# Gate and up products of a chunk as one block product, with a seven-product scheme in two of eight pairs of k tiles

## The chip, the cores and the metric

The kernel runs on one core of one Trainium2 chip. The metric is device microseconds (us) of one execution, lower is better. The engines named below are PE (matrix products; PEld is its weight load), DVE (vector), ACT (scalar), POOL and SP, whose queue here issues nearly all DMAs.

## The reference, cut to what matters

One decoder layer for 256 positions and 2048 channels: a gated feed-forward block (FFN), a mixer of two attention branches, and a second FFN. The change touches only the two FFNs, of which each computes

```python
def swiglu(h, w_gate, w_up, w_down):
    return (jax.nn.silu(h @ w_gate) * (h @ w_up)) @ w_down

x = x + 0.5 * swiglu(rms_norm(x, ffn1_norm), ffn1_w_gate, ffn1_w_up, ffn1_w_down)
```

with h of 256 x 2048, w_gate and w_up of 2048 x 5632, w_down of 5632 x 2048, all in float32.

## The kernel before

**Number format.** A product of float32 matrices is made of three PE products. Each operand is split in two parts of the type float32r: hi is the value copied to that type (ACT, line 98 for weights), lo is the value less hi (DVE, line 99). The product is then hi\*hi + hi\*lo + lo\*hi, three matmuls into the same PSUM tile (lines 114, 115 and 116). The x operand is split once per FFN (xh, xl, held with k along the partitions), the weights are split as they arrive.

**Tiles.** A k tile is 128 rows of a weight. A weight load (line 96, on SP's queue) brings two k tiles of 512 columns into one `raw` tile of 512 KB; four `raw` buffers exist (RAW_BUFS). A split pair (`w_hi`, `w_lo`) covers one `raw` tile; five such pairs exist (SPL_BUFS). One group is one such pair: two k tiles times two blocks of 128 positions (t = 0, 1) times three matmuls, so 12 matmuls of 128 x 128 weights (a block of x is the stationary operand) by 512 moving columns.

**An FFN.** `ffn` walks over 11 chunks of 512 columns of the gate and up weights in two halves (6 and 5 chunks). For each chunk, `linear` runs over the 8 groups of the gate weight into two PSUM tiles `mm` (one for each t), ACT applies Silu to them (line 254), `linear` runs over the 8 groups of the up weight into two more, and DVE multiplies both (line 258). `turn_blocks` then brings the result into k-major form: two DVE transposes (line 158), a DMA to DRAM (`blocks`, line 160) and one back (`moved`, line 163). Eight groups later (`defer(BLOCK_WAIT, ...)`) `split_blocks` splits it into `ah` and `al` (ACT line 131, DVE line 132). After a half's chunks, four `linear` calls with the down weight use `ah` and `al`.

**Order.** Each engine runs its own queue in the order that the framework fixed when the kernel was built; the framework also adds all waits between engines. A tile's buffer is reused once its last reader has finished. PSUM has eight banks: `ps_mm` four, `ps_tr` two, `ps_s` two.

Of the kernel before, what the change touches and what calls it, by code (L numbers as in the profile page):

```python
# [11 lines left out]
F32 = mybir.dt.float32  # L12
# [17 lines left out]
GRP = 2  # L30
RAW_BUFS = 4
SPL_BUFS = 5
HALVES = (6, 5)
DIL_G, DIL_H = 3, 4
DIFF_H = 4
# [16 lines left out]
def hybrid_layer_kernel(ctx: ExitStack, tc: tile.TileContext, a: dict, out: bass.AP):  # L52
# [23 lines left out]
    def tick():  # L76
        nonlocal groups
        groups += 1
        while later and later[0][0] <= groups:
            heapq.heappop(later)[2]()  # L80

    def flush():
        while later:
            heapq.heappop(later)[2]()

    def weight_groups(w, n0, nk):

        nonlocal last_hi, last_lo
        for k0 in range(0, nk, GRP):
            raw = wraw.tile([P, GRP, CH], F32, name="raw")  # L90
            hi = wspl.tile([P, GRP, CH], F32R, name="w_hi")
            lo = wspl.tile([P, GRP, CH], F32R, name="w_lo")
            step = 1 if groups == 0 else GRP
            for g in range(0, GRP, step):
                ks = slice(g, g + step)
                nc.sync.dma_start(raw[:, ks], w[(k0 + g) * P:(k0 + g + step) * P, n0:n0 + CH]  # L96
                                  .rearrange("(k p) n -> p k n", p=P))
                last_hi = nc.scalar.activation(hi[:, ks], raw[:, ks], AF.Copy)  # L98
                last_lo = nc.vector.tensor_tensor(lo[:, ks], raw[:, ks], hi[:, ks].bitcast(F32), op=ALU.subtract)  # L99
            yield k0, hi, lo  # L100

    def linear(w, n0, xh, xl, nk, ahead=None):

        ps = [ps_mm.tile([P, CH], F32, name="mm") for _ in range(NT)]
        for k0, hi, lo in weight_groups(w, n0, nk):
# [10 lines left out]
                    nc.tensor.matmul(ps[t], xl[:, k, sl], hi[:, kk], start=False, stop=k == nk - 1)  # L116
            tick()
        return ps

    def rsqrt_mean(ss, n, cols):  # L120

# [114 lines left out]
        return [rsqrt_mean(total(ss[t]), D, 1) for t in range(NT)]  # L236

    def ffn(wg, wu, wd, norm, done, ahead=None):
        with tc.tile_pool(name="act", bufs=1) as apool, tc.tile_pool(name="actw", bufs=2) as aw, \
                tc.tile_pool(name="actb", bufs=1) as bp:  # L240
            ah = apool.tile([P, 4 * HALVES[0], S], F32R, name="ah")
            al = apool.tile([P, 4 * HALVES[0], S], F32R, name="al")
            rs = None
            j = 0
            for half, count in enumerate(HALVES):
                down = wd[j * CH:(j + count) * CH]
                for i in range(count):
                    ps = linear(wg, j * CH, xh, xl, KD, ahead if j == 0 else None)
                    if rs is None:
                        rs = norm()  # L250
                    sg = []
                    for t in range(NT):
                        s = aw.tile([P, CH], F32, name="sg")
                        nc.scalar.activation(s, ps[t], AF.Silu, scale=rs[t])  # L254
                        sg.append(s)
                    ps = linear(wu, j * CH, xh, xl, KD)
                    for t in range(NT):
                        nc.vector.scalar_tensor_tensor(sg[t], ps[t], rs[t], sg[t], op0=ALU.mult, op1=ALU.mult)
                    x = turn_blocks(sg, bp)
                    defer(BLOCK_WAIT, lambda x=x, i=i: split_blocks(x, ah, al, 4 * i))  # L260
                    j += 1
                for n in range(D // CH):
                    ps = linear(down, n * CH, ah, al, 4 * count)
                    (done if half else part)(n, ps, bp)

    def part(n, ps, _):
# [461 lines left out]
```

## Time and profile before

| | us |
|---|---|
| median of 3 runs | 2147.96 (2147.25 to 2148.06) |
| the profiled execution | 2147.71 |
| its span in the profile | 2145.9 |
| PE busy in the span | 2133.2 |
| DVE busy | 1226.7 |
| ACT busy | 993.5 |

The span is what the profile covers; the profiled execution took 1.8 us more than its span. Busy times are sums over an engine's instructions. The granted clock of PE is full (1.00) in every stretch of this run. Matmul records overlap in time, because matmuls are pipelined, so the pace of matmuls is read from the distance between their starts and not from the length of one record.

### The profile page before, as it was taken

How to read it: one execution, taken by the hardware profiler on the slowest of the kernel's cores; microseconds unless marked ns; L12 is line 12 of the kernel's file. 1: busy time of each engine (PE TensorE's matmuls, PEld its weight loads, DVE VectorE, ACT ScalarE, POOL GpSimd, SP SyncE). 2: the span in 40 equal slices, each digit the busy share in tenths (PEclk: the TensorE clock that was granted, in tenths of full speed). 3: DMA queues.
4: the chain of work that ended last, by engine and by line, in shares of the span. 5: the costliest groups of instructions: out<-in, count | busy, mean ns of one | idle time of the engine just before them, and what ended most of it. 6: DMA issues, size and time to landing. Idle time of an engine off the chain costs nothing.

```text
span 2145.9 us, 25034 instructions
## 1 busy us (share of the span) xinstructions
PE 2133.2 (99%) x9490; PEld 1766.7 (82%) x9490; DVE 1226.7 (57%) x1456; ACT 993.5 (46%) x1193; POOL 47.7 (2%) x50
## 2 busy tenths in 40 slices
PE   8999999999999999999999999999999999999999
PEld 6888888888888888888888888888888888888887
DVE  5655554455556666767755566665555544555553
ACT  6445443444445545555556444454444433444442
POOL 0000000000000011010100000000000000000000
PEclk9999999999999999999999999999999999999999
DMA  7676665666667767666654567666666655676663
GB/s 251 215 230 216 215 214 191 193 216 212 219 216 245 246 196 234 227 215 213 205 181 157 196 222 244 220 226 215 210 223 215 223 192 193 198 229 212 213 230 134
DMA packets 241662, 456.25 MB, mean 213 GB/s; under 512 B 14162, under 2 KB 37252, under 8 KB 241284
## 3 DMA queue, kind: packets, MB, share of 16 engines
q1 hardware_dynamic: 241152, 454.09, 64.3%
q0 software_dynamic: 288, 0.53, 0.2%
q8 instruction: 74, 1.21, 0.2%
q14 instruction: 48, 0.39, 0.1%
q10 hardware_dynamic: 100, 0.03, 0.0%
HBM read 428.89 MB, written 25.69 MB: 212 GB/s over the span
## 4 chain that ended last, share of the span: by engine, by line
PE 99%; DMA 0%; DVE 0%; SPq 0%; issue 0%
PE mm L114 33%; PE mm L115 32%; PE mm L116 32%; PE s L581 0%; DMA xs<-in_x_dram 0%; PE tr L144 0%; PE s L500 0%; PE tr L610 0%; PE s L534 0%; PE tr L599 0%; PE tr L611 0%; PE tr L547 0%; DVE xs L695 0%; PE tr L522 0%; SPq L96 0%; SPq L225 0%
## 5 line engine op out<-in xcount | busy, mean ns | idle before, releaser
L99 DVE TENSOR_TENSOR w_lo<-raw,w_hi 128x1024 fp32r<-128x1024 f32 (+1 forms) x769 | 932.6, 1220 | 761.3 <-ACT w_hi L98 759.7
L98 ACT ACTIVATE w_hi<-raw 128x1024 fp32r<-128x1024 f32 (+1 forms) x769 | 807.8, 1057 | 910.1 <-PE mm L116 854.5
L114 PE MATMUL mm<-w_hi,xh 128*128 128x512 f32 x2144 | 837.0, 391 | 0.0
L115 PE MATMUL mm<-w_lo,xh 128*128 128x512 f32 x2144 | 836.4, 390 | 0.0
L116 PE MATMUL mm<-w_hi,xl 128*128 128x512 f32 x2144 | 833.9, 390 | 0.0
L116 PEld LDWEIGHTS mm<-w_hi,xl 128*128 128x128 f32 x2144 | 402.8, 188 | 83.5
L115 PEld LDWEIGHTS mm<-w_lo,xh 128*128 128x128 f32 x2144 | 402.8, 188 | 83.1
L114 PEld LDWEIGHTS mm<-w_hi,xh 128*128 128x128 f32 x2144 | 402.6, 188 | 83.1
L114 PE MATMUL mm<-w_hi,ah 128*128 128x512 f32 x704 | 273.9, 389 | 0.0
L115 PE MATMUL mm<-w_lo,ah 128*128 128x512 f32 x704 | 273.9, 389 | 0.0
L116 PE MATMUL mm<-w_hi,al 128*128 128x512 f32 x704 | 273.9, 389 | 0.0
L115 PEld LDWEIGHTS mm<-w_lo,ah 128*128 128x128 f32 x704 | 132.1, 188 | 27.5
L114 PEld LDWEIGHTS mm<-w_hi,ah 128*128 128x128 f32 x704 | 132.1, 188 | 27.5
L116 PEld LDWEIGHTS mm<-w_hi,al 128*128 128x128 f32 x704 | 132.1, 188 | 27.4
L132 DVE TENSOR_TENSOR al<-moved,ah 128x512 fp32r<-128x512 f32 x44 | 28.6, 688 | 75.2 <-ACT ah L131 75.2
L125 POOL TENSOR_TENSOR rr<-rv,mhalf 128x4 f32<-128x4 f32 (+1 forms) x34 | 41.6, 1226 | 1302.0 <-DVE rv L123 1302.0
L131 ACT ACTIVATE ah<-moved 128x512 fp32r<-128x512 f32 x44 | 25.4, 624 | 89.3 <-DMA moved<-blocks 89.3
L114 PE MATMUL mm<-w_hi,yh 128*128 128x512 f32 x128 | 49.9, 390 | 0.0
L116 PE MATMUL mm<-w_hi,yl 128*128 128x512 f32 x128 | 49.8, 389 | 0.0
L115 PE MATMUL mm<-w_lo,yh 128*128 128x512 f32 x128 | 49.8, 389 | 0.0
L158 DVE STREAM_TRANSPOSE turned<-sg 128x512 f32<-128x512 f32 x44 | 48.3, 1097 | 0.0
L254 ACT ACTIVATE sg<-mm,rr 128x512 f32<-128x512 f32 x44 | 29.8, 689 | 19.9 <-PE mm L116 19.9
(150 smaller groups left out, 750.6 us busy)
## 6 DMA issues: line engine op xcount, KB each, us to landing
raw<-in_w_in_dram SPq DMA_DIRECT2D x184, 512.0 KB, 3.6
raw<-in_ffn_w_up_dram SPq DMA_DIRECT2D x176, 512.0 KB, 4.6
raw<-in_ffn_w_down_dram SPq DMA_DIRECT2D x176, 512.0 KB, 4.5
raw<-in_ffn_w_gate_dram SPq DMA_DIRECT2D x175, 512.0 KB, 3.8
blocks<-turned SPq DMA_DIRECT2D x41, 512.0 KB, 4.4
raw<-in_w_out_dram SPq DMA_DIRECT2D x32, 512.0 KB, 5.2
moved<-blocks SPq DMA_DIRECT2D x31, 512.0 KB, 5.1
raw<-in_w_diff_branch_dram SPq DMA_DIRECT2D x16, 512.0 KB, 4.7
```

The source lines that it names most:

```text
L98: last_hi = nc.scalar.activation(hi[:, ks], raw[:, ks], AF.Copy)
L99: last_lo = nc.vector.tensor_tensor(lo[:, ks], raw[:, ks], hi[:, ks].bitcast(F32), op=ALU.subtract)
L114: nc.tensor.matmul(ps[t], xh[:, k, sl], hi[:, kk], start=k == 0, stop=False)
L115: nc.tensor.matmul(ps[t], xh[:, k, sl], lo[:, kk], start=False, stop=False)
L116: nc.tensor.matmul(ps[t], xl[:, k, sl], hi[:, kk], start=False, stop=k == nk - 1)
L125: nc.gpsimd.tensor_tensor(r, v, mhalf[:, :cols], op=ALU.pow)
L131: nc.scalar.activation(hi, src, AF.Copy)
L132: nc.vector.tensor_tensor(lo, src, hi.bitcast(F32), op=ALU.subtract)
L158: nc.vector.transpose(r[:, :, t], srcs[t].rearrange("p (kt i q) -> p q kt i", i=32, q=4))
L254: nc.scalar.activation(s, ps[t], AF.Silu, scale=rs[t])
```

## The change

Chunks 1 to 10 of each FFN no longer run gate and up one after the other: `two_chunks` takes the pair of gate and up columns (index i), the two blocks of positions (t) and the two k tiles of a pair (k) as a product of 2 x 2 by 2 x 2 blocks. There are eight pairs u = 0 to 7 of k tiles in a chunk. In six of them the eight block products are made as before, into four PSUM accumulators c00, c01, c10, c11 (first index t, second i), with three matmuls for each block product (`three`). In the pairs WINO = (3, 5) seven block products are made instead (p1, p5, p6, p7 go to four accumulators of their own, the others to c00, c01, c10), of sums and differences of blocks. The sums of x blocks are made once per FFN (`sums_of_x`), the sums of weight blocks (`t_a`, `t_b`) in each such pair, by DVE from `raw`, before they are split by `parts` like any weight. After pair 5, p1, p5, p6 and p7 are combined into e, u2, x, y, and at the end of the chunk the four c are added to these. All eight PSUM banks are in use; which four hold the c alternates from chunk to chunk. Silu now comes after the chunk's end, for both t. Chunk 0 runs as before. In the FFNs a sixth split pair exists (FFN_SPL).

```diff
+FFN_SPL = 1
+WINO = (3, 5)
...
+    def parts(src, n=GRP):
+        nonlocal last_hi, last_lo
+        hi, lo = split_tiles()
+        last_hi = nc.scalar.activation(hi[:, :n], src, AF.Copy)
+        last_lo = nc.vector.tensor_tensor(lo[:, :n], src, hi[:, :n].bitcast(F32), op=ALU.subtract)
+        return hi, lo
...
+    def three(ps, xs, ws, start, stop):
+        (h, l), (wh, wl) = xs, ws
+        nc.tensor.matmul(ps, h, wh, start=start, stop=False)
+        nc.tensor.matmul(ps, h, wl, start=False, stop=False)
+        nc.tensor.matmul(ps, l, wh, start=False, stop=stop)
...
+    def two_chunks(j, cols, xh, xl, nk, sx, tmp):
+        four = [ps_mm.tile([P, CH], F32, name="mm") for _ in range(4)]
+        def other():
+            tr = [ps_tr.tile([P, 2, S], F32, name="tr").rearrange("p a b -> p (a b)") for _ in range(2)]
+            sc = ps_s.tile([P, 2, CH], F32, name="s")
+            return [*tr, sc[:, 0], sc[:, 1]]
+        (c00, c01, c10, c11), (p1, p5, p6, p7) = (four, other()) if j % 2 else (other(), four)
...
+            if u not in sx:
+                for i in range(2):
+                    hi, lo = parts(raw[i])
+                    for k in range(2):
+                        for t in range(NT):
+                            three(c[t][i], op(k, t), (hi[:, k], lo[:, k]), u == 0 and k == 0, u == nu - 1 and k == 1)
+                    tick()
+                continue
...
+            b = parts(raw[0])
+            ta, tb = wtmp.tile([P, GRP, CH], F32, name="t_a"), wtmp.tile([P, GRP, CH], F32, name="t_b")
+            nc.vector.tensor_tensor(ta[:, 0], raw[1][:, 0], raw[0][:, 0], op=ALU.subtract)
+            nc.vector.tensor_tensor(ta[:, 1], raw[1][:, 0], raw[1][:, 1], op=ALU.subtract)
+            three(p1, op(0, 0), part(b, 0), st, sp)
+            three(c00, op(1, 0), part(b, 1), False, False)
+            b = parts(raw[1][:, 1:], 1)
+            three(c01, sm(3), part(b, 0), False, False)
+            nc.vector.tensor_tensor(tb[:, 0], raw[1][:, 1], ta[:, 0], op=ALU.subtract)
+            nc.vector.tensor_tensor(tb[:, 1], raw[0][:, 1], tb[:, 0], op=ALU.subtract)
+            tick()
+            b = parts(ta)
+            three(p5, sm(0), part(b, 0), st, sp)
+            three(p7, sm(2), part(b, 1), st, sp)
+            b = parts(tb)
+            three(p6, sm(1), part(b, 0), st, sp)
+            three(c10, op(1, 1), part(b, 1), False, False)
+            tick()
+            if sp:
+                nc.scalar.activation(e, p1, AF.Copy)
+                nc.vector.tensor_tensor(u2, p6, e, op=ALU.add)
+                nc.vector.tensor_tensor(x, p5, u2, op=ALU.add)
+                nc.vector.tensor_tensor(u2, p7, u2, op=ALU.add)
+                nc.vector.tensor_tensor(y, p7, x, op=ALU.add)
+        for acc, p in ((e, c00), (u2, c10), (x, c01), (y, c11)):
+            nc.vector.tensor_tensor(acc, p, acc, op=ALU.add)
+        return (e, x), (u2, y)
...
+                    if j == 0:
+                        ps = linear(wg, 0, xh, xl, KD, ahead)
+                        rs = norm()
...
+                        up = linear(wu, 0, xh, xl, KD)
+                        sx = sums_of_x(sxp, WINO)
+                    else:
+                        out = two_chunks(j, ((wg, j * CH), (wu, j * CH)), xh, xl, KD, sx, aw)
+                        sg, up = [o[0] for o in out], [o[1] for o in out]
+                        for t in range(NT):
+                            nc.scalar.activation(sg[t], sg[t], AF.Silu, scale=rs[t])
```

## Rows read from the trace of the kernel before

**Rows 1.** The page: span, busy time of engines, and the chain's shares by engine

```profile
span 2145.9 us, 25034 instructions
PE 2133.2 (99%) x9490; PEld 1766.7 (82%) x9490; DVE 1226.7 (57%) x1456; ACT 993.5 (46%) x1193; POOL 47.7 (2%) x50
PE 99%; DMA 0%; DVE 0%; SPq 0%; issue 0%
```

**Rows 2.** Waits of PE, whole span (us in total, times, longest)

```profile
PE tr L144 <- DMA xs<-in_x_dram: 4.5, 2, 4.3
PE tr L210 <- DMA g_raw<-in_ffn_norm_dram: 3.9, 1, 3.9
```

**Rows 3.** PE timeline in an FFN chunk: start us, length us

```profile
99.78 0.39 PE L114 MATMUL mm<-w_hi,xh 128*128 128x512 f32 x1
...
101.82 0.39 PE L114 MATMUL mm<-w_hi,xh 128*128 128x512 f32 x1
...
102.50 0.39 PE L114 MATMUL mm<-w_hi,xh 128*128 128x512 f32 x1
```

**Rows 4.** DVE groups by line and form: count, busy us, mean ns, idle before

```profile
L99 DVE TENSOR_TENSOR w_lo<-raw,w_hi 128x1024 fp32r<-128x1024 f32 x767 | 931.2, 1221 | 758.7 <-ACT w_hi L98 757.2
L158 DVE STREAM_TRANSPOSE turned<-sg 128x512 f32<-128x512 f32 x44 | 48.3, 1097 | 0.0
L258 DVE SCALAR_TENSOR_TENSOR sg<-mm,rr,sg 128x512 f32<-128x512 f32 x44 | 30.9, 742 | 0.0
L132 DVE TENSOR_TENSOR al<-moved,ah 128x512 fp32r<-128x512 f32 x44 | 28.6, 688 | 75.2 <-ACT ah L131 75.2
L446 DVE TENSOR_TENSOR q<-ra,rb 128x128 f32<-128x128 f32 x20 | 5.6, 280 | 0.0
L656 DVE TENSOR_TENSOR y<-mm,sig 128x512 f32<-128x512 f32 x8 | 5.1, 681 | 0.0
```

**Rows 5.** ACT groups by line and form, same columns

```profile
L98 ACT ACTIVATE w_hi<-raw 128x1024 fp32r<-128x1024 f32 x767 | 806.6, 1059 | 906.6 <-PE mm L116 854.5 <-DMA raw<-in_w_in_dram 25.7 <-DMA raw<-in_ffn_w_down_dram 6.6
L254 ACT ACTIVATE sg<-mm,rr 128x512 f32<-128x512 f32 x44 | 29.8, 689 | 19.9 <-PE mm L116 19.9
L131 ACT ACTIVATE ah<-moved 128x512 fp32r<-128x512 f32 x44 | 25.4, 624 | 89.3 <-DMA moved<-blocks 89.3
```

**Rows 6.** Timeline of DVE after a chunk: start us, length us, count, idle before

```profile
145.10 1.40 DVE L258 SCALAR_TENSOR_TENSOR sg<-mm,rr,sg 128x512 f32<-128x512 f32 x2
146.42 1.08 DVE L158 STREAM_TRANSPOSE turned<-sg 128x512 f32<-128x512 f32 x1
147.43 1.18 DVE L99 TENSOR_TENSOR w_lo<-raw,w_hi 128x1024 fp32r<-128x1024 f32 x1
148.53 1.10 DVE L158 STREAM_TRANSPOSE turned<-sg 128x512 f32<-128x512 f32 x1
...
161.70 3.50 DVE L99 TENSOR_TENSOR w_lo<-raw,w_hi 128x1024 fp32r<-128x1024 f32 x3 [0.18 <-ACT w_hi L98]
```

**Rows 7.** Timeline of ACT in the same stretch

```profile
153.69 1.06 ACT L98 ACTIVATE w_hi<-raw 128x1024 fp32r<-128x1024 f32 x1 [1.66 <-PE mm L116]
159.56 1.15 ACT L131 ACTIVATE ah<-moved 128x512 fp32r<-128x512 f32 x2 [4.80 <-DMA moved<-blocks]
160.62 2.94 ACT L98 ACTIVATE w_hi<-raw 128x1024 fp32r<-128x1024 f32 x3
```

**Rows 8.** Waits of ACT, whole span

```profile
ACT w_hi L98 <- PE mm L116: 854.5, 551, 3.0
ACT ah L131 <- DMA moved<-blocks: 89.3, 22, 5.1
```

**Rows 9.** Issue to landing, by tile `moved`, then by line 96 (weight loads)

```profile
DMA to landing us min/median/max: 3.8/5.1/7.0
...
DMA to landing us min/median/max: 3.3/4.3/10.5
```

**Rows 10.** A 5 us window; last columns: granted clock, DMA share, GB/s

```profile
165.00:170.00 5.00, 5.00 (x23) 4.14 (x23) 2.23 (x3) 4.13 (x5) 0.00 (x0) 1.00 0.96 311
```

More of the change, by code (lines that the diff above doesn't have):

```diff
@@ L84, in flush, with split_tiles @@
             heapq.heappop(later)[2]()
+    more_spl = []
+    wtmp = None
+    spl_turn = itertools.count()
+    def split_tiles():
+        pool = wspl
+        if more_spl and next(spl_turn) % (SPL_BUFS + FFN_SPL) >= SPL_BUFS:
+            pool = more_spl[0]
+        return pool.tile([P, GRP, CH], F32R, name="w_hi"), pool.tile([P, GRP, CH], F32R, name="w_lo")
+    def parts(src, n=GRP):
[4 more added lines that the diff above has]
+        return hi, lo
     def weight_groups(w, n0, nk):
@@ new lines, in two_chunks @@
+    def two_chunks(j, cols, xh, xl, nk, sx, tmp):
[5 more added lines that the diff above has]
+        (c00, c01, c10, c11), (p1, p5, p6, p7) = (four, other()) if j % 2 else (other(), four)
+        c = ((c00, c01), (c10, c11))
+        e, u2, x, y = (tmp.tile([P, CH], F32, name=n) for n in ("e", "u2", "x", "y"))
+        nu, first_sum, last_sum = nk // 2, min(sx), max(sx)
+        for u in range(nu):
+            raw = []
+            for w, n0 in cols:
+                r = wraw.tile([P, GRP, CH], F32, name="raw")
+                nc.sync.dma_start(r, w[2 * u * P:(2 * u + 2) * P, n0:n0 + CH].rearrange("(k p) n -> p k n", p=P))
+                raw.append(r)
+            op = lambda k, t: (xh[:, 2 * u + k, t * P:(t + 1) * P], xl[:, 2 * u + k, t * P:(t + 1) * P])
+            if u not in sx:
[6 more added lines that the diff above has]
+                continue
+            st, sp = u == first_sum, u == last_sum
+            sm = lambda i: (sx[u][0][:, i], sx[u][1][:, i])
+            part = lambda hl, k: (hl[0][:, k], hl[1][:, k])
+            b = parts(raw[0])
[25 more added lines that the diff above has]
+        return (e, x), (u2, y)
@@ L247, in ffn @@
                 for i in range(count):
-                    ps = linear(wg, j * CH, xh, xl, KD, ahead if j == 0 else None)
-                    if rs is None:
+                    if j == 0:
+                        ps = linear(wg, 0, xh, xl, KD, ahead)
                         rs = norm()
-                    sg = []
-                    for t in range(NT):
[L253 to L258, printed above, removed]
+                        sg = [aw.tile([P, CH], F32, name=n) for n in ("e", "u2")]
+                        for t in range(NT):
+                            nc.scalar.activation(sg[t], ps[t], AF.Silu, scale=rs[t])
+                        up = linear(wu, 0, xh, xl, KD)
[3 more added lines that the diff above has]
+                        sg, up = [o[0] for o in out], [o[1] for o in out]
+                        for t in range(NT):
+                            nc.scalar.activation(sg[t], sg[t], AF.Silu, scale=rs[t])
+                    for t in range(NT):
+                        nc.vector.scalar_tensor_tensor(sg[t], up[t], rs[t], sg[t], op0=ALU.mult, op1=ALU.mult)
                     x = turn_blocks(sg, bp)
```

30 lines of the change are left out of this document (25 added, 5 removed).

## Prediction

> **What bounds the kernel now.** I read the page first: PE is busy for 99% of the span, and the chain that ended last is PE for 99% [rows 1]. A busy PE is not yet a bound, so I read its waits next: two causes in the whole span, 8.4 us together, both at the start (gains and x on their way in) [rows 2]. From then on no matmul waited for a weight, a bank or a transposed block. The third view is the timeline of PE: four line-114 matmuls, which are 12 matmuls of all three lines, take 102.50 - 99.78 = 2.72 us [rows 3], so a matmul costs 226.7 ns and a group 2.72 us. Fourth, who waits for PE: ACT's hi waited for a PE matmul 551 times, 854.5 us [rows 8], that is, ACT stands ready and waits for a split buffer to come free. Weights are split ahead of need, and the number of buffers limits how far. So the time is the number of matmuls times 226.7 ns, as long as DVE, ACT and the loads keep that lead. DVE is 57% busy and ACT 46% [rows 1]; the change takes from PE and gives to both.
>
> **What it removes.** A pair of k tiles costs 8 block products x 3 = 24 matmuls, a pair of the new scheme 7 x 3 = 21 (p1, c00, c01, p5, p7, p6, c10). That is 3 less in each of 2 pairs of 10 chunks of 2 FFNs: 120 matmuls of the same shape, 120 x 0.2267 = 27.2 us, all on the path [rows 3]. A chunk goes from 192 x 0.2267 = 43.5 us to 186 x 0.2267 = 42.2 us, a scheme pair from 5.44 to 4.76 us. The banks change after every three matmuls as before, and so do the stationary blocks, so I keep the pace.
>
> **What it adds to DVE, for one chunk** (durations from [rows 4]; additions that read PSUM by the 681 ns of line 656, others by the 688 ns of line 132). Splits of full tiles: 12 in the six plain pairs and 3 in each scheme pair, 18 x 1.221 = 21.98. Half-tile splits: 2 x 0.688 = 1.38. The t_a and t_b sums: 8 x 0.688 = 5.50. Combining p's: 4 x 0.681 = 2.72. Adding c's: 4 x 0.681 = 2.72. Then as before: two multiplications 1.48, two transposes 2.19, two `al` splits 1.38. Sum 39.4 us, against 24.6 before (16 x 1.221 + 5.05). PE needs 42.2 us, so DVE fits with 2.8 us to spare, and 93% busy. Back to back it is cheaper: three splits took 3.50 us, not 3.66, and two multiplications 1.40, not 1.48 [rows 6], about 0.08 us saved per instruction; over the 42 of a chunk 3.4 us, so some 36.0 us. I take 36 to 39.4.
>
> Here the trace and a rule part. The Trainium skill, "VectorE: DVE Perf Modes", section "The DRAIN you can't avoid", says that an op is followed by a flush of the pipe before the next starts, and advises to keep the number of ops low, which speaks against this change. The overlapping starts in [rows 6] show less than that; by the rule the chunk's sum would stay at 39.4 us, by the rows it is 36.0.
>
> **ACT, for one chunk** [rows 5]: 18 x 1.059 + 2 x 0.63 + one copy of p1 0.69 + two Silu 1.38 + two `ah` 1.25 = 23.6 us of 42.2. It hides; the question is only what it waits for.
>
> **Local load.** Pairs 3 to 5 are the dense stretch. DVE: 2 x (3 x 1.221 + 5 x 0.688 = 7.10) + pair 4's 2.44 + `al` 1.38 + combining 2.72 = 20.7 us, PE 4.76 + 5.44 + 4.76 = 15.0. The lead has to cover 5.8 us. With six split buffers, tile n can be split when tile n-6 is done. In us from a chunk's start PE begins its split tiles at 0, 2.72, 5.44, 8.16, 10.88, 13.60 (pairs 0 to 2), 16.32, 17.68, 18.36, 19.72 (pair 3: 6, 3, 6 and 6 matmuls), 21.08 and 23.80 (pair 4), 26.52, 27.88, 28.56, 29.92 (pair 5). So pair 3's first tile may be split from 2.72, 13.6 us early, and pair 5's last must be there by 29.92. In these 27.2 us DVE has 18 us to do (20.7 less the combining). It is covered: 0.
>
> **What is queued behind the `ah` wait.** This is the narrowest place. `moved` comes late and ACT stands at line 131 for it, 22 times, 89.3 us [rows 8], and all splits queue behind. In the rows shown ACT took a hi at 153.69, waited 4.80 us, ran `ah` at 159.56 and then three hi without pause [rows 7]; DVE did three lo at once [rows 6]. The chunk's end was near 145.35 (101.82, where the chunk's first matmul starts [rows 3], plus 43.5), so `ah` ran 14.2 us after it. Now y's addition and the multiplications come after the last matmul, some 0.9 us later than the old multiplication (which began 0.25 us before the end), so `ah` runs at about 15.1 and ends at 16.3. In the shown chunk the hi just ahead of `ah` was the one released 8.3 us after the end; I take the same place, between the tiles released at 8.16 and 10.88. The next two hi then end at 17.3 and 18.4, their lo after the two `al` at about 18.5 and 19.7; PE wants these at 19.95 and 21.3 (one matmul behind the hi). Spare: 1.4 us. One place later it is 2.6; one place earlier the tile wanted at 18.6 comes at 18.5 and nothing is spare. `moved` lands in 3.8 to 7.0 us, median 5.1 [rows 9], so a slow one takes up to 1.9 us and can break through. This falls on 18 chunks (9 in each FFN). Bounds: 0, and 18 x 1.9 = 34 us. I take 0.2 us each, 3.6 us, near the lower end, since the median has room.
>
> **Edits at nothing.** `sums_of_x`: two times (2 x 0.688 + 4 x 0.28) = 5.0 us of DVE once per FFN, beside chunk 0's up products, where DVE has 43.5 - 24.6 = 19 us free; uncovered it would cost 5 us x 2. From chunk 0 to 1, the third accumulator needs the bank of up's first block, first at 0.68 us after the boundary; the multiplication that frees it starts 0.25 us before and takes 0.66 [rows 6]. From chunk 5 to the down product, banks of ps_mm are wanted at once; the gate accumulators have been complete for 12 matmuls (2.72 us), and if the second bank is c01's, it is complete 0.68 us before the end and wanted 0.68 us after, enough for one addition of 0.68; behind a split on DVE it costs up to 1.2 us, two times. The p's are free after pair 5 and wanted as c's a chunk later. The later Silu delays only the `ah` chain above. A slower shift in the weight pace would need matmuls that wait, which is the same matter.
>
> **The sum.** Against the profiled execution: 2147.71 = span 2145.9 + 1.8; 2145.9 - 27.2 + 3.6 = 2122.3, with 1.8 around it 2124.1. The median of the runs is 0.25 us above that execution, so **2124.4 us**. With nothing lost it would be 2120.8.
>
> **Rivals.**
>
> *Loads and late blocks eat part of it.* In a scheme pair both `raw` tiles stay occupied until t_b is made: hi 1.06, then DVE 1.22 + 5 x 0.688 = 4.66, so 5.7 us. Then two loads go out together; the first lands after 4.3 us [rows 9], the second 1.7 us later (512 KB at the 311 GB/s of a full stretch [rows 10]). That is 11.7 us around a loop of four buffers, which PE uses up in two pairs, 10.2 us. Each scheme pair so loses 1.5 us of lead, 3.0 per chunk, and `blocks` and `moved` use the same queue and rate. For it: the fourth buffer is exactly not enough here. Against: t_a and t_b need only `raw` and may run long ahead of the buffers for their splits, and plain pairs win the lead back. At 0.4 to 1.1 us per chunk over 20 chunks 8 to 22 us are lost: 2129 to 2143. Chance 0.23.
>
> *DVE becomes the bound; slower.* Place: the scheme pairs, where DVE makes sums, ACT copies them to hi, and DVE needs that hi again, four times in a pair. If queue order leaves each hand-off open, DVE stands still for 3 x 1.06 + 0.63 = 3.8 us per pair, 7.6 per chunk; 39.4 + 7.6 = 47.0 us against 42.2, so 4.8 us lost in each of 20 chunks: 2120.8 + 96 = 2217 us. It turns into a loss from 1.36 us per chunk (27.2 / 20), that is, from waits of 2.8 + 1.4 = 4.2 us in a chunk, somewhat over half of the hand-offs. For it: before, DVE's idle time ahead of lo is nearly all a wait for hi (758.7 us) [rows 4]. Against: that wait is ACT's own wait for a free buffer [rows 8], and while ACT makes one hi, DVE has the next sums or the last lo to do. Chance 0.13.
>
> *It does not do what it says.* Only if gaps of PE between small steps equal the matmuls saved, 0.68 us in a scheme pair: 2148, no change. It takes the same mechanisms at a chance strength; 0.07.
>
> **How the numbers follow.** The forecast, losses up to 8 us, holds 0.57: 2119 to 2129. With the first rival, faster is 0.57 + 0.23 = 0.80, less 0.02 of it that reaches within 0.2% (4.3 us, about what a measurement of this kernel can tell from no change): 0.78. Same: 0.07 + 0.02 = 0.09. Slower: 0.13. The range starts at 2118, the full saving and a little for the pace, and goes to 2146, so that it leaves out the slower rival and a part of the no-change case.
>
> **What would show it.** Right: PE has 120 instructions less, next to no idle time in chunks 1 to 10, the same 2.72 us for 12 matmuls; DVE's busy time up by some 20 x 14.8 + 10 = 306 us at its durations; `ah` waits about as long as before. Wrong in the `ah` step: PE idle at pair 3 or 4, released by lo, with ACT waiting for `moved` ahead of it. Wrong in the loads: ACT's hi waiting for `raw` transfers in pairs 5 to 7. Wrong in DVE's sum: PE idle behind lo in pairs 5 and 6, DVE without pauses or pausing for hi. A pace above 2.72 us without waits would upset the first term.

## The result and the profile after

| | before | after |
|---|---|---|
| median, us | 2147.86 (2147.25 to 2148.06) | 2133.65 (2133.20 to 2136.70) |
| the profiled execution | 2147.71 | 2133.20 |
| its span | 2145.9 | 2131.4 |
| DVE busy in the span | 1226.7 | 1482.3 |

The kernel became faster, by 14.2 us; the ratio after to before is 0.9937, with a 95% interval of 0.9925 to 0.9949. The forecast was 2124.4 us, 23.5 us faster. The direction was right and the time lies in the range; 9 us of the gain that was forecast are missing. Of the kernel under "Time without the wait" below, one execution in a slow state took 4333.4 us; its numbers are those of the other three.

The page of after, span, engines and shares of the chain (before: [rows 1]):

```profile
span 2131.4 us, 25439 instructions
PE 2112.3 (99%) x9370; PEld 1744.8 (82%) x9370; DVE 1482.3 (70%) x1880; ACT 1063.4 (50%) x1297; POOL 48.9 (2%) x50
PE 75%; DVE 11%; DMA 10%; issue 2%; ACT 1%; SPq 0%; DVEq 0%; ACTq 0%
```

PE ran 120 matmuls less, as forecast. It is 99% busy as before, but the chain that ended last is no longer PE alone: from some places it leads back through DVE and through a load. So PE waited somewhere for them. The waits of after, engine, line, releaser, then us in total, times and the longest (before: [rows 2], [rows 8]):

```profile
PE tr L143 <- DVE w_lo L103: 5.2, 4, 3.7
PE mm L133 <- DVE e L226: 1.8, 2, 1.0
DVE t_a L203 <- DMA raw<-in_ffn_w_up_dram: 82.1, 38, 3.8
DVE w_lo L103 <- ACT w_hi L102: 75.4, 71, 2.1
ACT ah L240 <- DMA moved<-blocks: 107.9, 22, 8.5
ACT w_hi L102 <- DVE t_b L210: 43.2, 12, 4.2
```

(Lines of after: 102 and 103 make the hi and lo of a weight in the new chunks, 142 to 144 are the three matmuls of a block product, 133 to 135 those of `linear`, 203 and 204 make `t_a`, 209 and 210 `t_b`, 226 adds the c at a chunk's end, 374 is the multiplication, 267 the transposes, 269 and 272 the DMAs of `blocks` and `moved`, 240 and 241 make `ah` and `al`.) PE's own waits are few. The largest new wait stands on DVE: the first `t_a` of a scheme pair waits for the load of the up weight, 38 times, 82.1 us. ACT's wait at `ah` grew from 89.3 to 107.9 us, its longest from 5.1 to 8.5.

Where the time went is seen by stretches. These windows are chunks 1 to 5 of the first FFN, then chunks 1 and 5 of the second. Columns are us, then busy time and instructions of PE, PEld, DVE, ACT and POOL, granted clock, DMA share, GB/s.

```profile
57.67:100.46 42.79, 42.79 (x188) 34.90 (x187) 32.31 (x48) 19.09 (x21) 2.54 (x4) 1.00 0.62 191
100.46:148.26 47.80, 44.12 (x187) 35.96 (x186) 41.65 (x82) 25.72 (x32) 0.00 (x0) 0.96 0.65 210
148.26:190.42 42.16, 42.16 (x187) 34.92 (x186) 36.64 (x45) 23.45 (x27) 0.00 (x0) 1.00 0.70 225
190.42:233.44 43.02, 42.60 (x187) 34.76 (x186) 36.59 (x44) 23.21 (x26) 0.00 (x0) 1.00 0.68 222
233.44:276.95 43.51, 42.73 (x187) 34.60 (x186) 36.50 (x44) 22.39 (x26) 0.00 (x0) 1.00 0.65 219
1462.87:1505.03 42.16, 42.16 (x187) 34.91 (x186) 34.52 (x40) 22.48 (x25) 0.00 (x0) 1.00 0.66 213
1632.09:1675.46 43.37, 42.33 (x188) 34.77 (x186) 35.97 (x43) 22.17 (x26) 0.00 (x0) 1.00 0.64 220
```

An undisturbed chunk takes 42.16 us, which is 186 x 0.2267, the forecast's number; 11 of the 20 chunks are like that. The other nine are longer, worked out from the starts of their first matmuls: in the first FFN chunk 1 by 0.6 us (0.4 of it is at the same place in before), chunk 2 by 5.6, chunks 4 and 5 by 0.9 and 1.3, chunks 9 and 10 by 0.7 and 1.0; in the second FFN chunks 4, 5 and 10 by 0.6, 1.2 and 1.2. That is 13.1 us, less the 0.4 of before 12.7. The full saving of 27.2 us less 12.7 is 14.5, and the span became 14.5 us shorter. The rest stayed as it was: chunk 1 of the first FFN begins at 57.67 us (57.90 before), the stage between the FFNs takes 689.53 us in both, and a down product 32.64 or 27.20 us per block of columns.

The largest loss, in chunk 2 of the first FFN, in the timelines of PE, ACT, SP and DVE (start us, length us, operation, count, idle before and its releaser):

```profile
121.62 0.39 PE L142 MATMUL tr<-w_hi,xh 128*128 128x512 f32 x1
125.68 0.80 PE L143 MATMUL tr<-w_lo,xh 128*128 128x512 f32 x1 [3.67 <-DVE w_lo L103]
...
126.70 0.63 PE L142 MATMUL s<-w_hi,xh 128*128 128x512 f32 x1
127.13 0.63 PE L143 MATMUL s<-w_lo,xh 128*128 128x512 f32 x1
...
129.20 0.39 PE L142 MATMUL s<-w_hi,xh 128*128 128x512 f32 x1
```

(a window of it, columns as above:)

```profile
127.00:128.00 1.00, 1.00 (x4) 0.71 (x4) 1.00 (x2) 1.00 (x2) 0.00 (x0) 0.50 0.84 268
```

```profile
115.68 1.04 ACT L102 ACTIVATE w_hi<-raw 128x1024 fp32r<-128x1024 f32 x1
125.16 1.15 ACT L240 ACTIVATE ah<-moved 128x512 fp32r<-128x512 f32 x2 [8.44 <-DMA moved<-blocks]
```

```profile
116.78 0.34 SPq L269 DMA_DIRECT2D blocks<-turned  x1
117.36 0.37 SPq L186 DMA_DIRECT2D raw<-in_ffn_w_up_dram  x1
121.14 0.37 SPq L272 DMA_DIRECT2D moved<-blocks  x1
```

```profile
105.51 0.68 DVE L226 TENSOR_TENSOR x<-mm,x 128x512 f32<-128x512 f32 x1
108.07 0.69 DVE L203 TENSOR_TENSOR t_a<-raw 128x512 f32<-128x512 f32 x1 [1.88 <-DMA raw<-in_ffn_w_up_dram]
...
109.29 0.68 DVE L226 TENSOR_TENSOR y<-mm,y 128x512 f32<-128x512 f32 x1
...
115.65 1.11 DVE L267 STREAM_TRANSPOSE turned<-u 128x512 f32<-128x512 f32 x1
116.68 0.65 DVE L103 TENSOR_TENSOR w_lo<-raw,w_hi 128x512 fp32r<-128x512 f32 x1
...
118.38 1.22 DVE L103 TENSOR_TENSOR w_lo<-t_b,w_hi 128x1024 fp32r<-128x1024 f32 x1
...
119.92 0.37 DVE L447 TENSOR_SCALAR ang<-freq,posf 128x16 f32<-128x16 f32 x2
123.11 0.69 DVE L203 TENSOR_TENSOR t_a<-raw 128x512 f32<-128x512 f32 x1 [2.82 <-DMA raw<-in_ffn_w_up_dram]
...
124.41 1.22 DVE L103 TENSOR_TENSOR w_lo<-raw,w_hi 128x1024 fp32r<-128x1024 f32 x1
```

Read from the bottom up. PE waits from 122.01 to 125.68 for a lo that DVE starts at 124.41. The hi of that lo had been done since 116.72 (ACT, 115.68 + 1.04); DVE had been free to make it from about 119.5, but for 0.8 us of the mixer's tables. But in DVE's queue the `t_a` of pair 5 stands ahead of it, and this waits for an up load that SP could issue only at 117.36, right after DVE's half-tile lo of pair 3 (116.68 + 0.65) had set a `raw` buffer free. So DVE's lateness came back to it through a late load. A `t_a` had waited in the same way some fifteen microseconds before: the chunk had ended at 100.46, its last accumulators were ready, and a `t_a` of the next chunk stood among the additions of c and waited 1.88 us for its load. Behind it came the addition of y, the multiplications and the transposes, all mixed with other sums and lo. So the block went out at 116.78, 16.3 us after the chunk's end, where in the shown chunk of before it went out 4.3 us after it. Only 1.88 us of these 16.3 is idle time of DVE; for the rest it worked on what stood ahead in its queue. ACT then stood 8.44 us at `ah`, with every later hi queued behind; the hi of the lo that PE waited for was done before. The stall of PE is 3.67 us by the records; the matmul at 125.68 starts 4.06 us after the one before it, 3.8 us late. The eight steps after it, up to 129.20, took 3.5 us instead of 1.8, most of them 0.43 us each, at a granted clock of half (0.50, the 1.2 GHz level), 1.7 us more. Together that is 5.5 of the 5.6 us of this chunk.

The other losses have the same form. In all seven chunks in which PE was held up before the chunk's end (2, 4, 5, 9 and 10 of the first FFN, 4 and 10 of the second; chunk 1 shows 0.1 us twice) it was so first at the same matmul, the first that reads a lo of pair 4, 21.1 us after the chunk's start. Each time the hi of that lo was done 4.7 to 7.7 us before the lo began, ahead of ACT's wait at `ah`, and the lo stood in DVE's queue behind the `t_a` of pair 5, which had waited 2.2 to 3.8 us for its up load. The two waits for `e` (chunk 5 of each FFN) are of another kind: a down product wants a bank whose c has not been added yet.

Over all 20 chunks the issue of `blocks` came, at the median, 4.3 us after the chunk's end before and 11.9 us after; `ah` began at 13.4 and at 20.3 us.

### The profile page after: what moved, and what is told of

Its sections match the earlier page's. It is cut to its first block, busy times and chain, and to the rows that moved or that the text cites. A ratio compares the mean times of both kernels' runs of the same rounds, so it can differ in the third digit from the quotient of the medians.

```text
span 2131.4 us, 25439 instructions
## 1 busy us (share of the span) xinstructions
PE 2112.3 (99%) x9370; PEld 1744.8 (82%) x9370; DVE 1482.3 (70%) x1880; ACT 1063.4 (50%) x1297; POOL 48.9 (2%) x50
## 4 chain that ended last, share of the span: by engine, by line
PE 75%; DVE 11%; DMA 10%; issue 2%; ACT 1%; SPq 0%; DVEq 0%; ACTq 0%
PE mm L133 19%; PE mm L134 19%; PE mm L135 19%; DMA raw<-in_ffn_w_up_dram 7%; DVE w_lo L103 6%; PE mm L143 2%; PE mm L144 2%; PE mm L142 2%; PE tr L143 2%; PE tr L144 2%; PE tr L142 2%; PE s L144 1%; PE s L143 1%; PE s L142 1%; DMA raw<-in_ffn_w_gate_dram 1%
## 5 line engine op out<-in xcount | busy, mean ns | idle before, releaser
L118 DVE TENSOR_TENSOR w_lo<-raw,w_hi 128x1024 fp32r<-128x1024 f32 (+1 forms) x449 | 543.3, 1218 | 379.1 <-ACT w_hi L117 377.2
L117 ACT ACTIVATE w_hi<-raw 128x1024 fp32r<-128x1024 f32 (+1 forms) x449 | 471.4, 1056 | 482.1 <-PE mm L135 400.8
L102 ACT ACTIVATE w_hi<-raw 128x1024 fp32r<-128x1024 f32 x320 | 316.4, 1003 | 222.9 <-DMA raw<-in_ffn_w_gate_dram 47.8
L103 DVE TENSOR_TENSOR w_lo<-raw,w_hi 128x1024 fp32r<-128x1024 f32 x320 | 361.9, 1150 | 71.0 <-ACT w_hi L102 69.7
L133 PE MATMUL mm<-w_hi,xh 128*128 128x512 f32 x864 | 339.4, 394 | 0.0
L134 PE MATMUL mm<-w_lo,xh 128*128 128x512 f32 x864 | 338.9, 393 | 0.0
L135 PE MATMUL mm<-w_hi,xl 128*128 128x512 f32 x864 | 336.4, 392 | 0.0
L143 PE MATMUL mm<-w_lo,xh 128*128 128x512 f32 x540 | 210.6, 390 | 0.3 <-DVE w_lo L103 0.3
L144 PE MATMUL mm<-w_hi,xl 128*128 128x512 f32 x540 | 210.1, 389 | 0.0
L142 PE MATMUL mm<-w_hi,xh 128*128 128x512 f32 x540 | 209.4, 389 | 0.0
L135 PEld LDWEIGHTS mm<-w_hi,xl 128*128 128x128 f32 x864 | 162.6, 188 | 33.6
L134 PEld LDWEIGHTS mm<-w_lo,xh 128*128 128x128 f32 x864 | 162.8, 188 | 33.3
L133 PEld LDWEIGHTS mm<-w_hi,xh 128*128 128x128 f32 x864 | 162.7, 189 | 33.3
L134 PEld LDWEIGHTS mm<-w_lo,ah 128*128 128x128 f32 x704 | 132.2, 188 | 27.2
L143 PEld LDWEIGHTS mm<-w_lo,xh 128*128 128x128 f32 x540 | 101.4, 188 | 22.9 <-DVE w_lo L103 1.9
L142 PEld LDWEIGHTS mm<-w_hi,xh 128*128 128x128 f32 x540 | 101.4, 188 | 21.1
L144 PEld LDWEIGHTS mm<-w_hi,xl 128*128 128x128 f32 x540 | 101.4, 188 | 20.9
```

The lines of the kernel that those rows point to most:

```text
L102: last_hi = nc.scalar.activation(hi[:, :n], src, AF.Copy)
L103: last_lo = nc.vector.tensor_tensor(lo[:, :n], src, hi[:, :n].bitcast(F32), op=ALU.subtract)
L133: nc.tensor.matmul(ps[t], xh[:, k, sl], hi[:, kk], start=k == 0, stop=False)
L134: nc.tensor.matmul(ps[t], xh[:, k, sl], lo[:, kk], start=False, stop=False)
L142: nc.tensor.matmul(ps, h, wh, start=start, stop=False)
L143: nc.tensor.matmul(ps, h, wl, start=False, stop=False)
```

## The experiments

Four causes were set against each other. One: **DVE's order**, that is, the sums stand in DVE's queue where they wait for a load, with work that is due behind them. Two: **L**, the loop of `raw` buffers (the first rival of the prediction). Three: **the place of `ah`**, the forecast's own narrow step. Four: **H**, the hand-offs between DVE and ACT (the second rival). Two smaller ones joined them: DVE's time as such, and the tables of the mixer that DVE and ACT prepare in chunk 2. The expectations call some of them by letters. All times are medians; the 2147 to 2148 us of before were measured beside each. The queues' order is made anew for every kernel, so an edit can change it besides what it is meant to change.

**Five split pairs, as in before.**

```diff
-FFN_SPL = 1
+FFN_SPL = 0
```

> The changed kernel without its sixth split pair in the FFNs (five split pairs, four raw buffers). Theory L (the loop of four raw buffers limits how far DVE and ACT run ahead: t_a waited 38 times for the up load, 82.1 us, and everything behind it on DVE came late): the sixth pair is hardly ever full, so the time moves little, 2132 to 2138 us. Theory S (the number of split pairs sets the lead): one tile less of lead in each of 20 chunks, over 5 us slower, 2139 us or more. Theory A (only the wait of ah for moved blocks costs): like S in direction, since the spare time before a late block shrinks by a tile: 2140 to 2155.

2130.0 us (2128.3 to 2131.5), ratio 0.9914 (0.9900 to 0.9929). Without the sixth pair the kernel is not slower; if anything a little faster. The losses move and shrink (chunk 2 now 3.2 us, chunk 4 1.8), and the waits at `t_a` fall to 36.2 us; the order of DVE's queue, built anew, is another one. So a sixth split pair is not what the time hangs on, and the total of the `t_a` waits isn't the loss either: it matters what is behind them.

**Six raw buffers, five split pairs.**

```diff
-FFN_SPL = 1
+FFN_SPL = 0
+FFN_RAW = 2
...
-            raw = wraw.tile([P, GRP, CH], F32, name="raw")
+            raw = raw_tile()
```

> The changed kernel with the same memory spent otherwise: the sixth split pair of the FFNs (8 KB per partition) is given up for a fifth and sixth raw buffer (4 KB each). Theory L: the waits of t_a for the up load go from 82.1 us to under 25, chunk 2 of FFN 1 loses its stall of some 5.6 us and chunks 4, 5, 9, 10 most of theirs but the bank wait of 1.0 us twice; 2121 to 2126 us. Theory S: slower than the changed kernel, as one split pair is missing: 2136 or more. Theory A: as the control with five split pairs and four raw buffers.

2131.5 us (2128.4 to 2133.8), ratio 0.9921 (0.9906 to 0.9935), against 0.9914 with four raw and as many split pairs. The waits at `t_a` are 30.3 us, but PE still loses about as much, now also behind hi:

```profile
PE mm L152 <- ACT w_hi L112: 3.4, 9, 0.9
```

L by itself gets no support: six buffers instead of four bought nothing, in the order that came with them. That the loop takes part is seen in chunk 2 of after, where the late up load waited for a buffer that DVE set free late.

**`ah` four groups later.**

```diff
-                    defer(BLOCK_WAIT, lambda x=x, i=i: split_blocks(x, ah, al, 4 * i))
+                    defer(BLOCK_WAIT + (4 if i < count - 1 else 0), lambda x=x, i=i: split_blocks(x, ah, al, 4 * i))
```

> The changed kernel with the split of the moved blocks placed 12 groups after its chunk instead of 8 (8 where a down product follows). Theory A (the prediction's step: ACT stands at ah for a late block and the splits behind it come late): ah waits (107.9 us in 22 before this edit) fall below 40 us and the stalls go but for the bank waits; 2122 to 2127 us. Theory L: the raw loop stays; DVE still waits for the up loads at t_a, the stalls move; 2130 to 2135.

2138.9 us (2132.8 to 2139.7), ratio 0.9948 (0.9931 to 0.9964): no gain. But the edit moved nothing: in the trace every engine has the same operations on the same tiles in the same order as in after, each `ah` has as many hi ahead of it, and ACT's wait there stayed at 108.5 us in 22 times. So a later `ah` was not tested; that it was not what held PE is read from the seven stalls above. In effect this is after measured a second time, 5.2 us longer by the medians. Differences of this size between kernels that lose time are not to be read as effects.

**Sums left out.** The splits take `raw` in their place.

```diff
-            nc.vector.tensor_tensor(ta[:, 0], raw[1][:, 0], raw[0][:, 0], op=ALU.subtract)
...
-            nc.vector.tensor_tensor(tb[:, 1], raw[0][:, 1], tb[:, 0], op=ALU.subtract)
...
-            b = parts(ta)
+            b = parts(raw[1])
...
-            b = parts(tb)
+            b = parts(raw[0])
```

> The changed kernel with the sums of weight blocks t_a and t_b left out: the scheme pairs split the raw tiles themselves in their place (same splits, same 21 matmuls per pair, other values). DVE has 8 instructions of 0.69 us less per chunk and a raw tile is needed by splits alone, one of them later than before. If DVE's load or the hold by t_a and t_b is the cause: 2121 to 2125 us. If raw buffers are held as long by the last split (theory L in its general form, the loop counts and not the sums): 2128 or more.

2121.3 us (2120.7 to 2122.6), ratio 0.9875 (0.9860 to 0.9890). The span is 2118.6 us, 27.3 below that of before: the whole saving of 120 matmuls. PE has no waits but the two at the start:

```profile
PE tr L248 <- DMA xs<-in_x_dram: 4.4, 2, 4.2
PE tr L314 <- DMA g_raw<-in_ffn_norm_dram: 3.8, 1, 3.8
```

So all that was lost comes with the four sums per scheme pair, and neither the additions of p and c, the later Silu, the eight banks nor the smaller tiles cost PE anything by themselves. `blocks` goes out 7.1 us after a chunk's end.

**Time without the wait.** The sums are made of x parts, which are there from the start; their results are unused.

```diff
-            nc.vector.tensor_tensor(ta[:, 0], raw[1][:, 0], raw[0][:, 0], op=ALU.subtract)
+            nc.vector.tensor_tensor(ta[:, 0].rearrange("p (k s) -> p k s", s=S), xh[:, 2 * u:2 * u + 2].bitcast(F32), xl[:, 2 * u:2 * u + 2].bitcast(F32), op=ALU.subtract)
```

> The changed kernel with the four sums per scheme pair computed from xh and xl instead of raw and not used (the pairs split raw tiles in their place): DVE has the same 160 instructions of 0.69 us, but none of them waits for a load and nobody waits for them. Theory D (DVE's time alone): 2128 to 2136 us as the changed kernel. Theories W (a sum stands in DVE's queue waiting for the up load, with ready splits behind it) and H (hand-off of t_a and t_b to ACT and back): 2120 to 2123 us.

2127.9 us (2127.8 to 2129.1), ratio 0.9914 (0.9894 to 0.9933): 6.6 us above the kernel without sums. It is not the even test of DVE's time that it was meant to be. As these sums wait for nothing, they came to stand far ahead in DVE's queue: those of a whole FFN are made in its chunks 0 to 3. The first sum of each pair (line 203; us, busy us and count on DVE, granted clock, DMA share, GB/s), in chunk 1 of the first FFN and from its chunk 4 to the end of the mixer:

```profile
59.27:101.42 42.15, 4.78 (x7) 1.00 0.58 188
190.51:1417.69 1227.18, 0.00 (x0) 1.00 0.66 216
```

Chunk 1 has seven of them instead of two, chunks 4 to 10 have none. Most of the loss lies in two chunks, 4.8 us in chunk 2 of the first FFN, after a block that went out 23.8 us after its chunk's end, and 1.6 in chunk 1 of the second. Eighteen chunks ran at the full pace, but fifteen of them hold no sums. So sums that wait for no load cost PE time as well, where they crowd ahead of work that is due. What DVE's time alone would cost with two pairs in every chunk is not shown.

**The wait without the time.** The sums cover 8 columns; their results are unused.

```diff
-            nc.vector.tensor_tensor(ta[:, 0], raw[1][:, 0], raw[0][:, 0], op=ALU.subtract)
+            nc.vector.tensor_tensor(ta[:, 0, :8], raw[1][:, 0, :8], raw[0][:, 0, :8], op=ALU.subtract)
```

> The changed kernel with sums of 8 columns instead of 512, not used (the pairs split raw tiles in their place): the same waits for both loads in DVE's queue at some 0.17 us each, and no hand-off. Theory W: the waits of t_a for the up load stay (82.1 us, 38 times in the changed kernel) and so do the losses: 2128 us or more. Theories D and H: 2120 to 2123 us.

2126.4 us (2124.7 to 2127.8), ratio 0.9904 (0.9889 to 0.9918): 5.1 us above the kernel without sums, from 46.3 us of waits at `t_a` and next to no time of DVE; `blocks` goes out 10.6 us after the end. So sums that wait cost by themselves too, nearly without their time. This and the 6.6 us of the kernel before are no two parts of the 12.4 us that separate after from the kernel without sums, since the sums stand at other places there.

**Sums in full, unused.** `t_a` and `t_b` are made, the splits take `raw`.

```diff
-            b = parts(ta)
+            b = parts(raw[1])
...
-            b = parts(tb)
+            b = parts(raw[0])
```

> The changed kernel with all four sums on DVE in full size and with their waits, but not used: the pairs split raw tiles in their place, so no hi waits for t_a or t_b. Theory H (hand-off): 2120 to 2124 us. If D and W together make the losses: 2128 to 2136 us as the changed kernel.

2174.5 us (2167.8 to 2177.8), ratio 1.0124 (1.0106 to 1.0142), slower than the kernel before the change. The hand-off from sum to hi is gone here, and the time rose by 41 us over after: H gets no support. But the edit does a second thing. The last two splits of a pair now read `raw`, so both buffers stay taken until after them, and the loads that need them can only go out later. `ah` waits 153.4 us, its longest 11.4:

```profile
ACT ah L240 <- DMA moved<-blocks: 153.4, 22, 11.4
PE mm L142 <- ACT w_hi L102: 14.8, 6, 4.5
```

It isn't a clean test of H. The kernels without sums and with sums of 8 columns hold `raw` just as long and lose 0 and 5.1 us, so the longer hold is not enough by itself; with the sums made in full it goes with 41 us more than in after. How much of these the hold makes up, and how much the order built anew, is not shown.

**Sums on POOL.**

```diff
-            nc.vector.tensor_tensor(ta[:, 0], raw[1][:, 0], raw[0][:, 0], op=ALU.subtract)
+            nc.gpsimd.tensor_tensor(ta[:, 0], raw[1][:, 0], raw[0][:, 0], op=ALU.subtract)
```

(and the other three likewise)

> The changed kernel with the four sums of weight blocks per scheme pair on POOL instead of DVE (POOL is busy 2% of the span). Without the sums the losses in the FFN chunks were gone, so they come from the sums on DVE. If it is DVE's time or the order of its queue (theories D and W), POOL takes both away: 2121 to 2125 us, unless POOL's sums are so slow that t_b comes too late for the hand-off to ACT (theory H): then ACT waits for t_b and the time is 2128 or more.

2179.7 us (2174.1 to 2182.4), ratio 1.0149 (1.0132 to 1.0166). Groups of DVE and POOL by line and form (count, busy us, mean ns, idle before), first after, then this kernel:

```profile
L103 DVE TENSOR_TENSOR w_lo<-raw,w_hi 128x1024 fp32r<-128x1024 f32 x280 | 336.8, 1217 | 71.0 <-ACT w_hi L102 69.7
L103 DVE TENSOR_TENSOR w_lo<-raw,w_hi 128x512 fp32r<-128x512 f32 x40 | 27.0, 675 | 0.0
L203 DVE TENSOR_TENSOR t_a<-raw 128x512 f32<-128x512 f32 x40 | 27.7, 692 | 82.1 <-DMA raw<-in_ffn_w_up_dram 82.1
```

```profile
L103 DVE TENSOR_TENSOR w_lo<-raw,w_hi 128x1024 fp32r<-128x1024 f32 x280 | 364.8, 1317 | 83.9 <-ACT w_hi L102 82.3
L103 DVE TENSOR_TENSOR w_lo<-raw,w_hi 128x512 fp32r<-128x512 f32 x40 | 40.0, 1000 | 4.6 <-ACT w_hi L102 4.6
L209 POOL TENSOR_TENSOR t_b<-raw,t_a 128x512 f32<-128x512 f32 x40 | 72.5, 1814 | 0.0
```

A sum takes 1.6 to 1.8 us on POOL instead of 0.69, and DVE's lo beside it take longer. DVE is rid of 160 sums and is nearly as busy as with them, 1473.4 us against 1482.3; without any sums it was 1397.1. Of these 76 us more, the lo make up 49 (364.8, 40.0 and 108.2 for the lo of the sums, against 436.5 and 27.3 without sums). So of the 85 us that the sums had added to DVE's busy time 76 came back, 49 of them in longer lo. How much of PE's loss comes from these, and how much from sums that take longer themselves, was not separated. The Trainium skill, "SBUF — State Buffer", section "Who interferes with whom", says that a DVE instruction with two SBUF inputs contends with a GpSimd instruction that reads SBUF; the longer lo agree with it.

**The mixer's tables later.** They are made during the first down product instead of chunk 2.

```diff
-    defer(20, other_gains)
+    defer(98, other_gains)
...
-    defer(34, table_loads)
-    defer(28, lambda: pinned(masks))
-    defer(40, lambda: pinned(rotary))
-    defer(48, lambda: pinned(head_gains))
+    defer(100, table_loads)
+    defer(106, lambda: pinned(masks))
+    defer(114, lambda: pinned(rotary))
+    defer(124, lambda: pinned(head_gains))
```

> The changed kernel with the tables of the mixer (masks, rotary, head gains, other gains) made during the first down product of FFN 1 and not in its chunks 1 to 3. If the stall of 5.6 us in chunk 2 of FFN 1 comes from these small DVE and ACT instructions on top of the sums: that chunk's loss falls below 1 us and the time to 2127 to 2130 us. If it comes from the sums and loads alone, the chunk keeps 3 us or more and the time stays at 2131 to 2136 us.

2132.8 us (2131.7 to 2134.8), ratio 0.9934 (0.9917 to 0.9950): the same as after. Chunk 2's loss fell from 5.6 to 0.6 us, but chunks 3 and 5 of the first FFN rose to 1.1 and 3.3, chunk 5 of the second to 2.5, and 1.6 us came up at the start of the first down product. The stalls inside chunks, again in seven, are at the same matmul of pair 4. The tables decided where the lead ran out, not whether it did.

**One scheme pair only, the later one.**

```diff
-WINO = (3, 5)
+WINO = (5,)
```

> The scheme in pair 5 alone: 60 matmuls less than before, 13.6 us. If each scheme pair costs DVE the same lead, the losses are half of the changed kernel's 12 us: 2140 us. If the losses come only when two scheme pairs follow closely (DVE's backlog of the first not yet gone), nothing but the bank wait of some 2 us and the tables in chunk 2 are left: 2135 to 2138 us.

2133.5 us (2133.4 to 2133.9), ratio 0.9937 (0.9922 to 0.9952). PE's waits are again the two at the start alone. Half the matmuls saved, 60 x 0.2267 = 13.6 us, arrive nearly in full (13.3 by the medians); after, with two pairs, arrives at the same time. In after the second pair earned its 13.6 us and lost about as much (12.7 by the chunks above).

**The scheme one pair later.**

```diff
-WINO = (3, 5)
+WINO = (4, 6)
```

> The scheme in pairs 4 and 6 instead of 3 and 5, one pair further from the stretch after a chunk's end in which DVE adds, multiplies and transposes. If the sums hurt because DVE makes them early, right in that stretch (theory W), this relieves it: 2126 to 2131 us. If it is DVE's total, or if combining p1, p5, p6, p7 so close to the chunk's end makes the next bank late: 2133 to 2140 us.

2123.1 us (2121.6 to 2123.8), ratio 0.9887 (0.9873 to 0.9902). Same number of instructions on PE, DVE and ACT, same buffers, 10.5 us faster than after, about twice the difference that a second measurement of after made, and with intervals that do not meet. `t_a` waits 22.3 us in 15 times instead of 82.1 in 38, and `blocks` goes out 8.7 us after a chunk's end. DVE's timeline around the end of chunk 4 of the second FFN, first after, then this kernel:

```profile
1632.61 0.68 DVE L226 TENSOR_TENSOR x<-tr,x 128x512 f32<-128x512 f32 x1
1635.94 0.69 DVE L203 TENSOR_TENSOR t_a<-raw 128x512 f32<-128x512 f32 x1 [2.66 <-DMA raw<-in_ffn_w_up_dram]
1636.56 0.68 DVE L204 TENSOR_TENSOR t_a<-raw 128x512 f32<-128x512 f32 x1
1637.16 0.68 DVE L226 TENSOR_TENSOR u<-s,u 128x512 f32<-128x512 f32 x1
```

```profile
1631.47 1.10 DVE L267 STREAM_TRANSPOSE turned<-e 128x512 f32<-128x512 f32 x1
1632.50 1.05 DVE L267 STREAM_TRANSPOSE turned<-u 128x512 f32<-128x512 f32 x1
1633.47 1.19 DVE L103 TENSOR_TENSOR w_lo<-raw,w_hi 128x1024 fp32r<-128x1024 f32 x1
1634.57 0.69 DVE L203 TENSOR_TENSOR t_a<-raw 128x512 f32<-128x512 f32 x1
```

In after `t_a` of pair 3 stands between the additions of c; here `t_a` of pair 4 comes after both transposes, and its load is there.

**That, with the tables later and another turn of the banks.** The chunk ahead of each down product then holds its c outside `ps_mm`.

```diff
-WINO = (3, 5)
+WINO = (4, 6)
...
-        (c00, c01, c10, c11), (p1, p5, p6, p7) = (four, other()) if j % 2 else (other(), four)
+        (c00, c01, c10, c11), (p1, p5, p6, p7) = (four, other()) if j in (2, 4, 7, 9) else (other(), four)
...
-    defer(20, other_gains)
+    defer(98, other_gains)
```

(and the other four `defer` as above)

> Pairs 4 and 6, the mixer's tables made during the first down product, and the banks dealt so that no down product's first bank was an accumulator c of the chunk just before it (chunks 5 and 10 keep their c in ps_tr and ps_s). With pairs 4 and 6 alone some 3.6 us were left: 1.7 in chunk 2 and 0.7 in chunk 3 of FFN 1, 1.1 in its chunk 5 (bank wait 1.0). If tables and banks are the causes of these: all chunks of both FFNs at their matmuls' 42.16 us, 2119 to 2121.5 us. If the sums still cost by themselves: the losses move to other chunks and the time stays at 2122 to 2125 us.

2120.9 us (2120.2 to 2121.5), ratio 0.9875 (0.9858 to 0.9891), faster than both kernels and as fast as the one without sums. It is 2.2 us under pairs 4 and 6 alone, with intervals that overlap, but by the chunks the 3.5 us that were left there are gone; tables and banks were not tried apart. All 20 chunks take 42.16 us, among them chunk 2 of the first FFN and chunk 5 of the second:

```profile
100.39:142.55 42.16, 42.16 (x187) 34.91 (x186) 36.38 (x43) 22.88 (x26) 0.00 (x0) 1.00 0.68 225
1622.42:1664.58 42.16, 42.16 (x188) 34.91 (x187) 36.58 (x43) 21.55 (x24) 0.00 (x0) 1.00 0.68 221
```

DVE does all its sums, 1486.8 us busy, and waits at `t_a` for 20.5 us. Nothing of this reaches PE.

## Why the prediction was right, and where it was not

**What it removes: right to 0.1 us.** 27.2 us were worked out; the kernel without sums gave 27.3 of span, and every undisturbed chunk took the 42.16 us. That smaller steps keep the pace was chosen without a row for it, and holds.

**What it adds to DVE: right, at the lower end or a little under it.** 36 to 39.4 us per chunk were given; the windows of chunks without other work show 34.5 to 36.6. The rule of the flush after each op, as the prediction took it from the Trainium skill ("VectorE: DVE Perf Modes", section "The DRAIN you can't avoid"), kept the sum at 39.4 and does not agree with these windows; the same section of the Trainium skill adds that a next op that is not held starts earlier, which they agree with. DVE's busy time rose by 255.6 us, not by the 306 that summed full durations: the overlap of some 0.08 us per instruction, which [rows 6] had shown, was left out of that check; over 424 more instructions it makes 34 of the 50 us between. ACT was given 23.6 us and shows 22.2 to 23.5 in chunks without other work.

**The local load "is covered: 0": this is the step that failed.** It counted split buffers and DVE's sums of durations over pairs 3 to 5, and found 18 us of work in 27.2 us. The sum is right, but additions of c, multiplications and transposes of the chunk before, 6.4 us by the prediction's own durations, fall into much the same time; with all of them it would be 24.4 of 27.2. And it let DVE take work in the order in which it was ready. DVE takes it in queue order, and there pair 3's sums of the next chunk came among the additions of c, the multiplications and the transposes, and pair 5's ahead of the first lo of pair 4, and waited there for a load. The second of these is where PE was held up, seven times. The prediction said of t_a that it "may run long ahead", and named that as an argument against the rival; running ahead was the harm, since what is ahead of its load blocks what is due.

**The `ah` step: its sign came, its cause did not.** It was called the narrowest place, and being wrong in it was to show as PE idle at pair 3 or 4, released by lo, with ACT waiting for `moved` ahead of it. The stalls at pair 4 look just so. But in all seven the hi was done before ACT came to `ah`, and the lo was held on DVE. As for the size, the step let `blocks` be 0.9 us later than before; it was 7.6 us later (11.9 against 4.3). `ah` was to begin 15.1 us after the end and began at 20.3. It took 0.2 us for each of 18 chunks, 3.6 us; the loss was 12.7 us, in nine chunks, 5.6 of them in one that a mean per chunk had no room for. So this term, the only one for losses in the sum, was mis-sized, and what filled it came from the step before it.

**Edits at nothing.** `sums_of_x`, the change from chunk 0 to 1 and the p's cost nothing. The bank wait from chunk 5 to the down product, for which 0 was taken with a cap of 1.2 us each, came: two waits, together 1.8 us, the longer 1.0. In the last kernel, with the banks turned the other way, it is gone; without sums it is gone too, with the banks as they were.

**The rivals.** Loads and late blocks was the nearest: its 2129 to 2143 hold the result, and the late blocks are in the trace. The band that the forecast gave to its own mechanism, 2119 to 2129, does not hold it; that the whole range does is owed to its width. But this rival's price came from four `raw` buffers, and six, with one split pair less, did not take the loss away. DVE as the bound through hand-offs did not come: ACT's wait for t_b is 43.2 us in 12 times, and the loss stayed below the 27.2 us from which it would have been slower. That it does nothing did not come.

**What is shown and what is only argued.** Shown: the sums cause all the loss; neither more raw buffers, fewer split pairs, nor the tables moved alone take it away; one pair, or both pairs moved by one, do or nearly do. A later `ah` was not tried, since that edit moved nothing. That pair 5's `t_a` stood ahead of pair 4's lo in each of the seven stalls is read from the trace. That the queue's order is the cause of all the rest was argued from the timelines and from the median lateness of `blocks`, which goes with the times (7.1 us without sums, 8.7 with pairs 4 and 6, 10.6 with waits alone, 11.9 in after), though not for all kernels: with sums of x parts it is 7.2, with five split pairs 8.1, and 7 to 9 us are lost nevertheless, and with the sums on POOL it is 7.5 where 58 us are lost. The median also hides the few chunks that count: of the 7.2, 23.8 and 24.2 us in two. Moving the pairs changes two things at once, where the sums stand and the order that is then built around them. A kernel with the same pairs and only another order on DVE was not run, so how much belongs to which stays open. More raw and six split pairs together were not tried.

## What to carry to other kernels

Work that fits into an engine's free time by its sum can still stop the bound engine: look where in the in-order queue the new instructions will stand, what they wait for there, and what is due behind them. Before adding buffers, move the new work by one stage, to where its input has surely arrived and the short deadlines are past; here that was worth 10.5 us, and two more buffers in place of a split pair nothing. See in the trace that an edit has moved what it was meant to move: one of these left the order as it was, another carried all its sums to the front. Try one unit of a repeated change first: one pair kept 13.3 of its 13.6 us, and showed that the trouble did not come with the scheme as such.

## What the runs showed of the hardware

After the one wait of 3.67 us PE came back at half the granted clock (0.50): matmuls 0.43 us apart instead of 0.227, until 129.20. The stall so cost 1.7 us beyond itself, nearly half as much again. Ahead of it PE had run without a pause. In before, too, the first matmuls of the run, behind a wait of 4.34 us, start 0.43 us apart (11.04, 11.46, 11.89), the pace that goes with 0.50 above, though the clock column says 1.00 there. So the clock was not full in every stretch of that run; the full pace begins at about 12.9 us.

With the sums on POOL, DVE's half-tile lo rose from 675 to 1000 ns and the lo of full `raw` tiles from 1217 to 1317 ns; a subtraction of 128x512 took 1.57 to 1.81 us on POOL by the profile.

The page's share of PE says 99% for both kernels: the 12.7 us lost are 0.6% of the span, and matmul records are 0.39 us long at a pace of 0.227, so delays below some 0.16 us are not counted as idle at all. The distance between the first matmuls of chunks showed them.
